# A hybrid encoder layer on one core: the forgetting-attention stage reordered, a fifth head's queries and keys computed in the first stage, and the small loads of that stage issued by GpSimd

## The chip, the cores and the metric

The kernel runs on one NeuronCore of a Trainium2 chip. The metric is the device time of one execution in microseconds (us); the time of a kernel is the median of its runs. The engines are named as the profile names them: PE is TensorE (PEld its weight loads), DVE VectorE, ACT ScalarE, POOL GpSimd, SP SyncE.

## The reference

One layer is computed for two groups of tokens together: 512 prompt tokens and 8 x 16 sample tokens, 640 columns in all, with a model width of 2048.

```
z = x @ w_in                       # queries, keys, values, gates, DeltaNet inputs, merge gates
branch A (FoX, 8 heads of 128):    s = q k^T * scale + (c_q - c_k), causal; softmax; p v
    sample tokens attend to a cache of 512 past rows per group and to themselves
branch B (gated DeltaNet, 8 heads): conv, normalise, chunked delta rule
y = sig(gA) * (A_out * silu(gate)) @ w_out_fox + sig(gB) * (B_out * silu(gate)) @ w_out_gdn
x1 = LayerNorm(alpha * x + y @ w_out)
out = x1 + sigmoid(x1 @ w_pl_gate) * RMSNorm(p @ w_pl_proj)
```

The keys, values, log forget values and DeltaNet states are outputs too. Everything is float32.

## The kernel before, in words

**Matrix products.** A float32 product is made of three products in the fast float32 format: weights and inputs are each split into a rounded part (`wh`, `xh`, cast by ACT) and a remainder (`wl`, `xl`, subtracted by DVE), and the sum wh·xh + wh·xl + wl·xh is accumulated. The 640 columns are two halves of 320. A block of 128 output rows is called a column of weights: 16 contraction steps x 2 halves x 3 products = 96 matmuls of 128x320, at lines L396 and L397 (`column`). Two columns can instead be made as a pair at L474 (`pair`), by a scheme with seven products in place of eight: 7 products x 8 steps x 3 = 168 matmuls of 128x320 in place of 192. A pair needs sums of weight tiles, made by DVE (L319). For some later pairs the sums are made ahead by POOL from tiles that SP loads and stores again (`weight_sums`, L291, L295, L301).

**Stages.** `front` computes the first columns, all gates and values, 22 merge gates, and queries and keys of four heads (`APART`), the last of these as pairs; queries and keys go to DRAM (`qkd`). `phase_fox` has the rest of the columns (`column`), among which the eight attention heads are spread, and the projection `proj` of the per-layer embedding. `phase_gdn` has the DeltaNet heads, spread among the columns that they need, and `tail` has the output projections.

**Order.** The program is written out by hand: the matmuls of the columns go on, and after every second step `tick` runs through the lanes, which are generators that emit a part of a head and say how long to wait. A model of the engines (`saw`) keeps `self.clock`, the time of PE by the model; a lane goes on when the clock has reached its time, when `self.now` (the count of ticks) allows, and when the PSUM banks of the stage's small products (`sps`, three of them) are modelled as read (`banks_free`). `self.every = 2` lets a lane step on every second tick. A step that yields a negative number waits until the model has its engines done less 1.5 us.

**A head.** `fox_all` takes a head when its queries and keys are ready and the head before the last is done. `fox_in` loads the gate (`sg`) and the values (`vn`), and has POOL copy the sample queries into `qpad`. For each of four blocks of 128 prompt queries, `scores` makes the scores (L754 for the first block, L388 to L390 for the others), DVE adds the bias `nb`, ACT takes exp; `fox_step` scales them (`softmax2`), transposes them (L726), copies them (L729), multiplies them with the values (L742). `fox_dec` does the sample tokens against the cache: scores with `kc` (L773) and with their own keys (L776), softmax, transposes (L793, L799), copies by ACT to `ppad` (L795) and `pn` (L801), products with `vc` (L813). `fox_out` transposes its result and stores the head.

**Loads.** All loads of this stage are issued by SP in one order with the weights (`wr`, L269): queries and keys (L1529), bias (L637, L639), gate (L665), values (L633), four tiles of 512 KB of the cache's keys and four of its values per head (L627). The tiles of `phase_fox` lie where those of `front` were, so its first memset and first loads wait until the last stores of `front` have landed.

Of the kernel before, what the change touches and what calls it, by code (L numbers as in the profile page):

```python
# [52 lines left out]
class Kernel:  # L53
# [9 lines left out]
    APART = 2, 3, 5, 6  # L63
    NG = 8
    PAIR0, PAIRS = 6, NG + 2 + FRONT // 2 + len(APART)
    BETWEEN = 3, 6
# [6 lines left out]
    def __init__(self, tc, ins, outs):  # L73
        self.clock, self.busy, self.wrote, self.paced = 0.0, [0.0, 0.0, 0.0], {}, False
        self.tc, self.nc, self.i, self.o = tc, tc.nc, ins, outs
        self.lanes, self.every = [], 2
        self.banks, self.read, self.nbanks = [], {}, 3
        self.now = 0


    def saw(self, ins):


        if ins.engine not in ENGINES or not ins.outs or not hasattr(ins.outs[0], "ap"):
            return
# [22 lines left out]
    def watch(self, gen):  # L108
# [7 lines left out]
        return abs(n), t + (0.25 if n > 0 else -1.5)  # L116
# [513 lines left out]
    def load_v(self, h):  # L630

        self.vn[h] = self.zt([P, 5, P], "vn", 2)
        self.nc.sync.dma_start(out=self.vn[h], in_=self.vd[:, :, h * P:(h + 1) * P].rearrange("t p d -> p t d"))  # L633

    def load_bias(self, h):
        nb = self.zt([P, T], "nb", 2)
        self.nc.sync.dma_start(out=nb, in_=bcast(self.rd[h], T, P))  # L637
        nbd = self.zt([P, NPT], "nbd", 2)
        self.nc.sync.dma_start(out=nbd, in_=bass.AP(self.sfd.tensor, self.sfd[h * 8].offset,  # L639
# [3 lines left out]
    def softmax1(self, xs, n):  # L643
# [3 lines left out]
        nm = self.zt([P, 1], "nm", 6)  # L647
        nc.vector.reduce_max(out=nm, in_=xs[:, 0:n], axis=AX.X, negate=True)
        sm = self.zt([P, 1], "sm", 6)
# [9 lines left out]
    def fox_in(self, h, q):  # L659

        nc = self.nc
        if h == 0:
            self.load_bias(0)
# [3 lines left out]
        if h == 0:  # L667
            for j in range(4):
                self.load_kv(0, "k", j)

# [12 lines left out]

    def fox_all(self):


        flow = [None] * 4
        for h in range(H):
            while h not in self.heads or self.heads[h][2] > self.now or min(self.outdone, self.decdone) < h - 2:
# [3 lines left out]
            q, k, _ = self.heads.pop(h)  # L693
            self.fox_in(h, q)
            if h == 0:
                yield 5
                for j in range(4):
                    self.load_kv(0, "v", j)
                yield 4
            parts = None  # L700
            for i in range(4):
                self.fox_step(flow)
                flow[0] = h, i, self.scores(h, i, q, k, parts)
# [14 lines left out]
    def fox_step(self, flow):  # L718

        nc = self.nc  # L720
        spread = weigh = None
        if flow[1]:
            h, i, (xs, _) = flow[1]
# [7 lines left out]
        if flow[0]:  # L731
            h, i, (xs, sm) = flow[0]
            self.softmax2(xs, P * (i + 1), sm)
            weigh = flow[0]
        if flow[2]:
            h, i, pT = flow[2]
            if i == 0:
                self.og = self.zt([P, T], "og", 2)
            vn, sl = self.vn[h], slice(i * P, (i + 1) * P)
            ops = self.sps()  # L740
            for kb in range(i + 1):
                nc.tensor.matmul(ops[:, 0:P], vn[:, kb, :], pT[:, kb * P:(kb + 1) * P], start=(kb == 0), stop=(kb == i))  # L742
            nc.vector.tensor_tensor(out=self.og[:, sl], in0=ops[:, 0:P], in1=self.sg[h][:, sl], op=ALU.mult)
            if i == 3:
                self.outs["gens"].append(self.fox_out(h, self.sg[h], self.og))
        flow[:] = None, weigh, spread, None

    def scores(self, h, i, q, k, parts):
# [9 lines left out]
        xs = self.zt([P, NPT], "xs", 3)  # L758
# [5 lines left out]
    def fox_dec(self, h, q, k):  # L764
# [12 lines left out]
        xd = self.zt([P, T], "xd")  # L777
# [12 lines left out]
        yield -2  # L790
        pt = self.dps()
# [6 lines left out]
        pt = self.sps()  # L798
        nc.tensor.transpose(pt[:, 0:P], xd[:, NPT:T], self.ident)  # L799
        pn = self.zt([P, P], "sq", 2, "pn")  # L800
        nc.scalar.copy(out=pn, in_=pt[:, 0:P])  # L801
        yield 4
# [418 lines left out]
    def run(self, ctx):  # L1221
# [18 lines left out]
        self.qkd = {(h, i): dr([P, T], F32, name=f"qkd{h}{i}") for h in (0, *self.APART) for i in range(2)}  # L1240
# [7 lines left out]
        self.outs, self.decs = self.lane(), self.lane()  # L1248
# [35 lines left out]
    def front(self, work):  # L1284
# [179 lines left out]
        def weights():  # L1464
# [3 lines left out]
            yield from self.weight_sums([t[:, x:x + 256] for t in ws for x in (0, 256)], slice(0, 12), (6, 4, 2))  # L1468
# [33 lines left out]
    def phase_fox(self, work):  # L1502
# [6 lines left out]
        self.heads, self.sg = {}, {}  # L1509
# [4 lines left out]
        ws = self.zt([P, 1024], "ws")  # L1514
        self.sums["gens"].append(self.weight_sums([ws[:, x:x + 256] for x in range(0, 1024, 256)], slice(12, 13),
                                                  (9, 7, 5, 20)))
        for h in range(H):
            qk = []
            if h in self.BETWEEN:
                self.mcol("eacc")  # L1520
            for c in range(2):
                stored = (h, c) in self.qkd
                if not stored:
                    acc = self.column()[0]
                self.until(lambda: min(self.qkdone) >= h - 2)
                x = self.zt([P, T], "qk"[c], 2)
                qk.append(x)
                if stored:
                    nc.sync.dma_start(out=x, in_=self.qkd[h, c])  # L1529
                    continue  # L1530
                for hf in range(2):
                    sl = slice(hf * HALF, (hf + 1) * HALF)
# [941 lines left out]
```

## Time and profile before

| | us |
|---|---|
| three runs | 2170.36, 2176.83, 2175.85 |
| median | 2175.85 |
| profiled execution | 2173.18 |
| its span, first to last instruction | 2171.3 |
| PE busy in the span | 2149.0 |

The profile's page has the busy time of each engine, the span in 40 slices, the DMA queues, the chain of work that ended last, the costliest groups of instructions and the DMA issues. A row of a window gives, after its limits and its length, the busy us and the number of instructions of PE, PEld, DVE, ACT and POOL, then the granted PE clock, the mean busy share of the 16 DMA engines and GB/s. A row of a timeline gives start, duration, engine, line, operation, tiles, and in brackets how long the engine had been idle and what ended it. `front` ends and `phase_fox` begins at 721.92 us of the span; `phase_fox` ends near 976 us.

### The profile page before, as it was taken

The page shows a single profiled execution, that of the slowest core. Times are in us where ns is not written, and L with a number is a line of the kernel's source. Part 1 is how long each engine was busy: PE and PEld are TensorE (multiplying, and loading weights), DVE is VectorE, ACT ScalarE, POOL GpSimd, SP SyncE. Part 2 cuts the span into 40 slices and gives each one's busy share as a digit, 9 for nine tenths or more (in the row PEclk, how much of TensorE's full clock was granted, in tenths as well). Part 3 has the DMA queues.
Part 4 walks back from the last instruction along what each step waited for, and adds up shares of the span by engine and source line. Part 5 has one row for each costly group of instructions (what it writes and reads, how often), then busy time and mean ns, then how long its engine had stood idle before and what let it go on. Part 6 is the DMA issues. An engine that isn't in the chain of part 4 may idle for free.

```text
span 2171.3 us, 41951 instructions
## 1 busy us (share of the span) xinstructions
PE 2149.0 (99%) x15438; PEld 2082.3 (96%) x15438; DVE 1566.0 (72%) x3207; ACT 1007.3 (46%) x2213; POOL 401.9 (19%) x596
## 2 busy tenths in 40 slices
PE   9999999999999999999999999999999999999998
PEld 7799999999999998899999999999999999999998
DVE  5877776767776565566478677766757787789987
ACT  4344443443444343353655566655443343354544
POOL 0022233323330101002334333332000000021100
PEclk9999999999999999999999999999999999999999
DMA  6356656666554899869978778878567656673465
GB/s 235 101 184 202 189 182 199 198 199 194 184 180 158 276 325 344 314 199 291 241 179 199 180 188 194 189 182 248 161 229 260 209 171 202 201 276 122 153 227 173
DMA packets 240670, 452.65 MB, mean 208 GB/s; under 512 B 38920, under 2 KB 122504, under 8 KB 240464
## 3 DMA queue, kind: packets, MB, share of 16 engines
q1 hardware_dynamic: 224912, 421.64, 59.5%
q0 software_dynamic: 15552, 28.32, 8.0%
q8 instruction: 122, 2.00, 0.4%
q14 instruction: 84, 0.69, 0.1%
HBM read 353.48 MB, written 96.38 MB: 207 GB/s over the span
## 4 chain that ended last, share of the span: by engine, by line
PE 91%; DVE 3%; DMA 3%; ACT 1%; SPq 0%; issue 0%; POOL 0%; ACTq 0%; DVEq 0%; POOLq 0%
PE g L474 44%; PE g L396 18%; PE g L397 18%; PE g L440 2%; PE s L974 1%; PE s L742 1%; PE s L813 1%; PE s L773 1%; DMA ws138b<-ws 0%; PE s L440 0%; PE s L1168 0%; DMA nb<-rd 0%; DVE sx L1006 0%; DVE sx L1004 0%; PE s L726 0%
## 5 line engine op out<-in xcount | busy, mean ns | idle before, releaser
L329 ACT CAST wh<-wr 128x512 fp32r<-128x512 f32 x624 | 381.2, 619 | 288.7 <-PE g L474 109.5
L335 DVE TENSOR_TENSOR wl<-wr,wh 128x512 fp32r<-128x512 f32 x516 | 358.3, 708 | 183.5 <-ACT wh L329 173.7
L474 PE MATMUL g<-xh,wh 128*128 128x320 f32 (+1 forms) x1296 | 402.9, 311 | 2.7 <-ACT m L1278 1.6
L474 PE MATMUL g<-xl,wh 128*128 128x320 f32 (+1 forms) x1296 | 401.2, 310 | 0.6 <-DVE xl L371 0.6
L474 PE MATMUL g<-xh,wl 128*128 128x320 f32 (+1 forms) x1296 | 401.4, 310 | 0.0
L396 PE MATMUL g<-xh,wh 128*128 128x320 f32 (+1 forms) x960 | 313.0, 326 | 0.7 <-ACT wh L329 0.7
L396 PE MATMUL g<-xh,wl 128*128 128x320 f32 (+1 forms) x960 | 297.1, 309 | 0.8 <-DMA wl<-in_w 0.7
L396 PE MATMUL g<-xl,wh 128*128 128x320 f32 (+1 forms) x960 | 297.2, 310 | 0.4 <-DVE xl L371 0.4
L397 PE MATMUL g<-xh,wh 128*128 128x320 f32 x960 | 297.3, 310 | 0.0
L397 PE MATMUL g<-xl,wh 128*128 128x320 f32 x960 | 297.0, 309 | 0.0
L397 PE MATMUL g<-xh,wl 128*128 128x320 f32 x960 | 296.7, 309 | 0.0
L474 PEld LDWEIGHTS g<-xh,wh 128*128 128x128 f32 x1296 | 243.9, 188 | 4.3 <-ACT m L1278 2.1
L474 PEld LDWEIGHTS g<-xl,wh 128*128 128x128 f32 x1296 | 243.7, 188 | 1.1 <-DVE xl L371 1.1
L474 PEld LDWEIGHTS g<-xh,wl 128*128 128x128 f32 x1296 | 244.1, 188 | 0.0
L474 PE MATMUL g<-t,wh 128*128 128x320 f32 (+1 forms) x1088 | 241.4, 310 | 0.0
L335 DVE TENSOR_TENSOR wl<-sr,wh 128x512 fp32r<-128x512 f32 x200 | 147.9, 759 | 98.6 <-ACT wh L329 97.6
L295 POOL TENSOR_TENSOR ws<-ws 128x171 f32<-128x171 f32 (+2 forms) x152 | 116.7, 768 | 541.5 <-DMA ws<-in_w 535.7
L396 PEld LDWEIGHTS g<-xh,wh 128*128 128x128 f32 x960 | 180.9, 188 | 11.9 <-issue 7.1
L474 PEld LDWEIGHTS g<-t,wh 128*128 128x128 f32 x1088 | 181.9, 188 | 0.6 <-issue 0.3
L396 PEld LDWEIGHTS g<-xh,wl 128*128 128x128 f32 x960 | 180.6, 188 | 1.4 <-DMA wl<-in_w 1.0
L397 PEld LDWEIGHTS g<-xh,wh 128*128 128x128 f32 x960 | 181.0, 189 | 0.9
L396 PEld LDWEIGHTS g<-xl,wh 128*128 128x128 f32 x960 | 180.9, 188 | 1.0 <-DVE xl L371 1.0
(440 smaller groups left out, 4148.8 us busy)
## 6 DMA issues: line engine op xcount, KB each, us to landing
wr<-in_w SPq DMA_DIRECT2D x252, 512.0 KB
wl<-in_w POOLq DMA_DIRECT2D x108, 256.0 KB, 5.8
kc<-in_kc SPq DMA_DIRECT2D x32, 512.0 KB
vc<-in_vc SPq DMA_DIRECT2D x32, 512.0 KB
sr<-in_w SPq DMA_DIRECT2D x25, 512.0 KB
ws<-in_w SPq DMA_DIRECT2D x96, 128.0 KB
sb<-in_w SPq DMA_DIRECT2D x80, 128.0 KB
md<-m SPq DMA_DIRECT2D x32, 320.0 KB
```

What stands on the lines that cost most here:

```text
L295: nc.gpsimd.tensor_tensor(out=o, in0=x, in1=y, op=op)
L329: nc.scalar.copy(out=hi, in_=src)
L335: nc.vector.tensor_tensor(out=lo, in0=src, in1=hi.bitcast(F32), op=ALU.subtract)
L396: nc.tensor.matmul(ps[0], whl[w], xhl[o][:, a], start=(first and x == 0), stop=(last and x == 2))
L397: nc.tensor.matmul(ps[1], whl[w], xhl[o][:, b], start=(first and x == 0), stop=(last and x == 2))
L440: nc.tensor.matmul(ps, x[:, sl], w, start=(s == 0 and n == 0), stop=(s == 15 and n == 2))
L474: nc.tensor.matmul(ps, a[:, w], b, start=(k == 0 and n == 0 and not more), stop=(k == last and n == 2), skip_group_check=True)
L742: nc.tensor.matmul(ops[:, 0:P], vn[:, kb, :], pT[:, kb * P:(kb + 1) * P], start=(kb == 0), stop=(kb == i))
L773: nc.tensor.matmul(s1[32 * j:32 * j + 32, :], self.qpad[:, 2 * j + par, :], kc[:, (j % 2) * NPT:(j % 2 + 1) * NPT], start=(par == 0), stop ...
L813: nc.tensor.matmul(od[32 * j:32 * j + 32, 0:P], self.ppad[:, c, 2 * j + par, :], vc[:, o:o + P], start=False, stop=(par == 1 and c == 3), ...
L974: nc.tensor.matmul(pp[:, o:o + 256].rearrange("p (a b) -> p a b", a=2), kq[:, 0, x], kq[:, :, x], start=True, stop=True)
```

## The change

- `APART` has five heads (1, 2, 3, 6, 7) in place of four; `front` has one pair more, `phase_fox` two columns fewer. Queries and keys of heads 4 and 5 are computed in `phase_fox` (`JOBS`) and go to DRAM as well. Head 0's were stored at the start, as before.
- The loads of `q`, `k`, `nb`, `nbd`, `sg` and `vn` are issued by POOL. The cache tiles, weights and stores stay with SP.
- At the start of `phase_fox`, head 0's queries, keys, bias and its eight cache tiles, and head 1's queries and keys, are all asked for at once. Head 0 may begin 5 us of the model's clock after that, a later head 7 us after its load, and at least 21.5 us (`PACE`) after the head before.
- In this stage a lane may step on every tick (`every = 1`) and a negative yield waits until the engines are done by the model (`lead = 0`).
- The step of a head is cut differently: transposes, then the product with the values, then the new scores, then the scaling of the scores before. The end of the sample tokens is a lane of its own (`fox_dec2`), with the small transpose and its copy `pn` ahead of the large ones.
- The 13th of the sums of weights made by POOL is made in `front` in place of `phase_fox`. `proj` starts with three tiles for its results and gets four more when head 7 is done.
- The model no longer counts DMA issues as work (`saw`).

The diff, cut to its core:

```diff
-    APART = 2, 3, 5, 6
     NG = 8
+    APART = 1, 2, 3, 6, 7
-    BETWEEN = 3, 6
+    PACE = 21.5
+    JOBS = 4, 5, None, None
...
-        return abs(n), t + (0.25 if n > 0 else -1.5)
+        return abs(n), t + (0.25 if n > 0 else -self.lead)
...
-        self.nc.sync.dma_start(out=self.vn[h], in_=self.vd[:, :, h * P:(h + 1) * P].rearrange("t p d -> p t d"))
+        self.nc.gpsimd.dma_start(out=self.vn[h], in_=self.vd[:, :, h * P:(h + 1) * P].rearrange("t p d -> p t d"))
...
-        nc.sync.dma_start(out=self.sg[h], in_=self.sgf[h])
+        nc.gpsimd.dma_start(out=self.sg[h], in_=self.sgf[h])
...
+    def load_qk(self, h):
+        qk = []
+        for c in range(2):
+            qk.append(self.zt([P, T], "qk"[c], 2))
+            self.nc.gpsimd.dma_start(out=qk[c], in_=self.qkd[h, c])
+        self.heads[h] = *qk, self.clock + (7 if h else 5)
+
     def fox_all(self):
-        flow = [None] * 4
+        flow, begun = [None] * 5, 0.0
+        self.load_qk(0)
+        self.load_bias(0)
+        for j in range(4):
+            self.load_kv(0, "k", j)
+        self.load_qk(1)
+        for j in range(4):
+            self.load_kv(0, "v", j)
         for h in range(H):
-            while h not in self.heads or self.heads[h][2] > self.now or min(self.outdone, self.decdone) < h - 2:
+            while h not in self.heads or max(self.heads[h][2], begun + self.PACE) > self.clock or min(self.outdone, self.decdone) < h - 2:
...
-                    while self.qkdone[1] < h - 1:
+                    while self.qkdone[1] < h - 1 or h + 1 not in self.kept:
                         yield 1
                     self.load_bias(h + 1)
+                    if h:
+                        self.load_qk(h + 1)
...
+        self.decs2["gens"].append(self.fox_dec2(h, xd))
+
+    def fox_dec2(self, h, xd):
+        nc = self.nc
+        pt = self.sps()
+        nc.tensor.transpose(pt[:, 0:P], xd[:, NPT:T], self.ident)
+        pn = self.zt([P, P], "sq", 2, "pn")
+        nc.scalar.copy(out=pn, in_=pt[:, 0:P])
         pt = self.dps()
...
+        self.every, self.lead = 1, 0.0
         work["gens"].append(self.fox_all())
```

**How the order moves.** First SP, where `front` ends and `phase_fox` begins (`qkd` and `out_fk` are the last stores of `front`). Before:

```order
L1457 DMA qkd_194<-m_1170 128x640
L1459 DMA out_fk<-m_1170 128x640
L1457 DMA qkd_193<-m_1169 128x640
L1529 DMA q<-qkd_185 128x640
L1529 DMA k<-qkd_186 128x640
L269 DMA wr<-in_w 128x1024 x2
L637 DMA nb<-rd 128x640
L639 DMA nbd<-sfd 128x1x512
L665 DMA sg<-sgf_169 128x640
L633 DMA vn<-vd 128x5x128
L627 DMA kc<-in_kc 128x1024 x4
```

Now:

```order
L1468 DMA qkd_200<-m_1176 128x640
L1470 DMA out_fk<-m_1176 128x640
L1468 DMA qkd_199<-m_1175 128x640
L628 DMA kc<-in_kc 128x1024 x4
L628 DMA vc<-in_vc 128x1024 x4
L270 DMA wr<-in_w 128x1024 x3
```

The small loads have left SP's order, and eight cache loads stand ahead of three weight loads. They stand on POOL now, at the same place:

```order
L1517 MEMSET qpad 128x256
L1518 MEMSET ppad 128x1024
L683 DMA q<-qkd_185 128x640
L683 DMA k<-qkd_186 128x640
L638 DMA nb<-rd 128x640
L640 DMA nbd<-sfd 128x1x512
L683 DMA q<-qkd_187 128x640
L683 DMA k<-qkd_188 128x640
L664 DMA sg<-sgf_169 128x640
L634 DMA vn<-vd 128x5x128
L667 COPY qpad<-q 128x4x16 x2
```

Head 0's queries and keys stand behind both memsets of POOL; before, SP issued these loads, and the memsets stood on another engine. On PE the first scores of head 0 (`s<-k,q`) stood behind 120 matmuls of columns from the start of `phase_fox`. Now, with the first row the last matmul of `front`, and 42 matmuls of columns from the second row to the row ahead of the scores:

```order
L475 MATMUL g<-xh,wl 128x320
L397 MATMUL g<-xh,wh 128x320
L398 MATMUL g<-xh,wh 128x320
...
L397 MATMUL g<-xh,wl 128x320
L398 MATMUL g<-xh,wl 128x320
L761 MATMUL s<-k,q 128x128
L397 MATMUL g<-xh,wh 128x320
L398 MATMUL g<-xh,wh 128x320
```

So the first head stands 78 matmuls earlier. Between the first scores of one head and those of the next there were 84, 84, 84, 120, 84, 84 and 120 matmuls of columns; there are now 108, 66, 84, 78, 84, 78 and 78.

On ACT, within a head, before (`pn` behind the two copies to `ppad`):

```order
L795 COPY ppad<-s 128x16x16 x2
L801 COPY pn<-s 128x128
L729 COPY pT<-s 128x128
L650 ACTIVATE xs,sm<-xs,nm 128x384
L329 CAST wh<-wr 128x512
```

Now:

```order
L805 COPY pn<-s 128x128
L810 COPY ppad<-s 128x16x16 x2
L735 COPY pT<-s 128x256
L651 ACTIVATE xs_9381,sm<-xs_9381,nm 128x512
L827 COPY on<-s 128x128
```

The copy that empties the PSUM bank `s` now goes ahead of the two that empty another bank.

More of the change, by code (lines that the diff above doesn't have):

```diff
@@ L81, in saw @@
     def saw(self, ins):
-        if ins.engine not in ENGINES or not ins.outs or not hasattr(ins.outs[0], "ap"):
+        if ins.engine not in ENGINES or "DMA" in type(ins).__name__ or not ins.outs or not hasattr(ins.outs[0], "ap"):
             return
@@ L693, in fox_all @@
             q, k, _ = self.heads.pop(h)
+            begun = self.clock
             self.fox_in(h, q)
[L695 to L699, printed above, removed]
             parts = None
             for i in range(4):
-                self.fox_step(flow)
-                flow[0] = h, i, self.scores(h, i, q, k, parts)
+                self.fox_step(flow, (h, i, q, k, parts))
                 if i == 0:
@@ L1239, in run @@
         self.sgd = self.sgf[H:]
-        self.qkd = {(h, i): dr([P, T], F32, name=f"qkd{h}{i}") for h in (0, *self.APART) for i in range(2)}
+        self.qkd = {(h, i): dr([P, T], F32, name=f"qkd{h}{i}") for h in range(H) for i in range(2)}
         self.vd = dr([5, P, 1024], F32, name="vd")
@@ L1513, in phase_fox @@
         self.vn = {}
[L1514 to L1519, printed above, removed]
-                self.mcol("eacc")
[L1521 to L1532, printed above, removed]
-                    if c == 0:
-                        nc.scalar.mul(x[:, sl], acc[hf], FOX_SCALE)
-                    else:
-                        nc.scalar.copy(out=x[:, sl], in_=acc[hf])
-                if c:
-                    nc.sync.dma_start(out=self.o["fk"][h], in_=x)
-            self.heads[h] = *qk, self.now + (9 if stored else 1)
@@ L1563, in phase_fox @@
         nc.sync.dma_start(out=self.sqd, in_=self.eacc)
+        self.every, self.lead = 2, 1.5
     def mcol(self, tag, **kw):
@@ L1779, in e_evac @@
         if n == 0:
[L1781 removed]
+            self.until(lambda: self.qkdone[1] == 7 and not self.sums["gens"])
             self.eacc = self.zt([P, T], "eacc")
[L1783 to L1784 removed]
+            tiles = [self.zt([P, 1024], "kc", 4, "e")[:, 0:T] for _ in range(4)]
+            self.e_tiles, self.q_tiles = tiles[0:3], [tiles[3]] * 2
             self.esq = None
+        if n == 3:
+            self.until(lambda: self.decdone == 7)
+            tiles = [self.zt([P, 1024], "vc", 4, "e")[:, 0:T] for _ in range(4)]
+            self.e_tiles, self.q_tiles[1] = [*self.e_tiles, *tiles[0:3]], tiles[3]
         e = self.e_tiles[n % len(self.e_tiles)]
@@ L2383, in _layout @@
     rest = iter(m[nf:nf + 3])
-    for h in range(1, H):
-        bl += [next(rest) for _ in range(h in Kernel.BETWEEN)]
-        if h not in Kernel.APART:
-            bl += [bq[h], bk[h]]
+    for h in Kernel.JOBS:
+        bl += [next(rest)] if h is None else [bq[h], bk[h]]
     bl += rest
```

93 lines of the change are left out of this document (49 added, 44 removed).

## The prediction

> **What bounds the kernel now.** I read the busy times first, then the chain that ended last, then the windows stage by stage.
>
> ```profile
> PE 2149.0 (99%) x15438; PEld 2082.3 (96%) x15438; DVE 1566.0 (72%) x3207; ACT 1007.3 (46%) x2213; POOL 401.9 (19%) x596
> PE 91%; DVE 3%; DMA 3%; ACT 1%; SPq 0%; issue 0%; POOL 0%; ACTq 0%; DVEq 0%; POOLq 0%
> 400.00:450.00 50.00, 50.00 (x343) 50.00 (x342) 35.34 (x48) 20.25 (x38) 15.43 (x15) 1.00 0.61 195
> 736.00:950.00 214.00, 211.01 (x1913) 192.76 (x1912) 131.50 (x313) 87.65 (x229) 16.28 (x30) 1.00 0.87 311
> 850.00:900.00 50.00, 48.42 (x446) 43.40 (x444) 32.92 (x82) 18.74 (x52) 4.57 (x8) 1.00 1.01 360
> ```
>
> PE is busy 99% of the span and holds 91% of the chain. So the time is PE's work plus PE's waits, and every other engine counts only where PE waits for it. The third row (a stretch of `front`) gives the price of a matmul of 128x320: 50 us / 343 = 0.146 us. The fourth and fifth rows are the attention stage: PE idles 3.0 us of 214 by this count, and the DMA engines are nearly full (share 0.87, in one stretch 1.01, at 360 GB/s). The waits of PE in this stage, and the one late load that the chain runs through there:
>
> ```profile
> PE s L754 <- ACT pn L801: 0.8, 1, 0.8
> PE s L388 <- ACT pn L801: 0.8, 1, 0.8
> PE s L388 <- DVE xd L780: 0.7, 2, 0.5
> PE s L754 <- ACT k L1536: 0.3, 1, 0.3
> PE s L388 <- ACT pT L729: 0.3, 1, 0.3
> 850.12 9.15 DMA nb<-rd
> ```
>
> They come to 2.9 us. The reader should see that this is nearly all that a better order of the heads can win: the heads already hide behind the columns.
>
> **The change part by part.** *Matmuls removed.* Queries and keys of one more head are made as a pair: 168 matmuls in place of 192. 24 x 0.146 = **-3.5 us**. The number and shapes of all other matmuls stay as they were, so this is all of PE's work that goes. The pair's extra sums and casts are DVE and ACT work in `front`, where DVE is busy 35.34 of 50 us and ACT 20.25: covered, and if they were not, the loss would show as PE waits, of which 400 to 450 has none.
>
> *Waits in the heads.* `pn` now goes ahead of the two `ppad` copies, which is what the two rows of 0.8 us wait for; fewer columns of queries and keys are left to empty (0.3); with `lead = 0` a step stands where the model has the engines done. The 0.7 us on `xd` stay likely, since the first head still has its cache scores and the next large scores without columns between. I take away 2.9 - 0.7 = 2.2 and add about 1.0 for what the view doesn't count: it shows a matmul as 0.31 us long though the next starts after 0.146, so each of six waits is some 0.16 longer than shown. **-3.2 us**, bounds 0 (new waits as large as the old ones, since 66 to 84 matmuls now lie between most heads) and -4.
>
> *Head 0 moved forward.* This is the large term on the other side. Here are the end of `front` on PE, SP's last store, POOL's memsets and the first scores before:
>
> ```profile
> 721.92 0.31 PE L396 MATMUL g<-xh,wh 128*128 128x320 f32 x1
> 724.43 0.32 SPq L1457 DMA_DIRECT2D qkd<-m  x1
> 726.66 0.32 SPq L1529 DMA_DIRECT2D q<-qkd  x1
> 726.71 0.31 POOL L1506 MEMSET qpad<- 128x256 f32 x1 [77.27 <-DMA qkd<-m]
> 726.96 0.95 POOL L1507 MEMSET ppad<- 128x1024 f32 x1
> 729.65 0.89 POOL L672 COPY qpad<-q 128x64 f32<-128x64 f32 x2 [1.73 <-DMA q<-qkd]
> 739.53 0.38 PE L754 MATMUL s<-k,q 128*128 128x128 f32 x2
> ```
>
> Call 721.92 zero. The memory of `phase_fox` is free when the last store of `front` has landed: 726.71 - 721.92 = 4.8. Before, the first scores stood at 17.6 (120 matmuls x 0.146) and found their loads long landed. Now they stand behind 42 matmuls: 42 x 0.146 = 6.1. And the loads that they need are issued by POOL behind its two memsets, which end at 726.96 + 0.95 - 721.92 = 6.0. What an issue by POOL costs is shown by the only DMAs that POOL issues in this kernel, the weight remainders of the DeltaNet stage (first row: the issue, least, median and most in ns; second: from issue to landing in us):
>
> ```profile
> L342 POOL DMA_DIRECT2D wl<-in_w x108: 847/865/1194, 1012.6 to 1493.2; - x108
> DMA to landing us min/median/max: 3.6/5.8/9.2
> ```
>
> The queries are issued at 6.0, the keys at 6.0 + 0.87 = 6.9, and the keys land at 6.9 + 5.8 = 12.7. PE reaches them at 6.1: **+6.5 us** of waiting. The bounds: as quick as SP's load of the same tile, 729.65 - 726.66 = 3.0, gives 9.9, a wait of 3.7; the slowest landing, 9.2 (the bias load in the chain took 9.15 too), gives 16.1, a wait of 9.9. I take the median, because eight cache loads of 512 KB are asked for from 4.8 on and fill the DMA engines as they are filled where those 108 ran. Nothing can run ahead of it: PE goes in order, the columns stand behind the scores, and DVE and ACT wait for the columns' banks. Head 0's bias, third on POOL, lands some 0.9 us after the keys and delays DVE, not PE: the next scores are 24 matmuls (3.5 us) on. `qpad` follows eight issues (6.0 + 8 x 0.87 = 13.0), and its reader, PE's cache scores, stands after the wait too.
>
> The Trainium skill, "DMA: Bandwidth & Descriptors", in the section on the anatomy of a DMA issued by GpSimd, gives 2.0 us plus the bytes at 436 GB/s; for 320 KB that is an estimate of 2.75 us, with which the wait would be 3.5 and the sum 3.0 us lower. The 108 rows above, of 256 KB, disagree with it in a filled stage, and the measured ones decide.
>
> *The clock behind the wait.* One wait of PE in the trace was followed by a slower granted clock, another wasn't:
>
> ```profile
> 1447.48 0.38 PE L1196 MATMUL s<-vr,uu 128*128 128x128 f32 x1 [1.92 <-DVE uu L1074]
> 1448.00:1451.00 3.00, 3.00 (x13) 3.00 (x13) 2.90 (x8) 2.16 (x4) 0.17 (x1) 0.50 1.08 275
> 1451.00:1455.00 4.00, 4.00 (x31) 3.99 (x30) 3.65 (x15) 0.41 (x2) 0.69 (x1) 0.94 0.91 206
> 99.77 0.42 PE L474 MATMUL g<-xh,wh 128*128 128x320 f32 x1 [1.65 <-ACT m L1278]
> 99.00:102.40 3.40, 2.63 (x18) 2.63 (x19) 2.79 (x5) 0.65 (x2) 0.00 (x0) 1.00 0.41 154
> ```
>
> After 1.92 us idle the clock was 0.50 for 3 us and 0.94 over the next 4: 3 x 0.50 + 4 x 0.06 = 1.7 us lost. After 1.65 us it stayed at 1.00. A wait of 6.5 us is longer than both: **+1.7 us**, bounds 0 (as behind the 1.65) and twice that (it is three times the 1.92). The Trainium skill, "TensorE: Matmul & The Clock Gate", in its part on the clock gate, says that the clock is halved after an idle window of about 3.4 us and comes back after as long a busy one; the rows agree with the half clock, and by that rule the price lies between the one I take and its double.
>
> *At nothing.* The 48 DMAs that POOL now issues are 48 x 0.87 = 42 us of an engine that is busy 16.28 us of 214; uncovered, they would delay `qpad`. The 13th sum of weights falls into the end of `front`, where POOL is idle:
>
> ```profile
> 650.00:700.00 50.00, 50.00 (x342) 50.00 (x342) 34.30 (x50) 20.22 (x37) 0.00 (x0) 1.00 0.40 135
> 731.44 4.67 SPq L627 DMA_DIRECT2D kc<-in_kc  x4
> 737.62 3.33 SPq L627 DMA_DIRECT2D vc<-in_vc  x4
> ```
>
> The three weight loads that now stand behind eight cache loads wait 4.67 + 3.33 = 8.0 us longer for their issue; by the order of SP four halves of columns (4 x 48 matmuls = 28 us) are issued ahead of them, which covers that and 4.2 MB in front (12 us at 360 GB/s). Without this cover it would be PE that waits for `wh`. The end of the stage is covered too: behind the last product of head 7 there are 25 us of columns ahead of the next stage's first small product, where there were 35. Fewer result tiles in `proj` and shared buffers hang on stores that have several columns' time. The DeltaNet stage keeps its work, but its order shifts a little where it follows the sums; its waits may fall better or worse, by about the 1.92 + 1.7 of the event above either way. I take 0.
>
> *The sum*: -3.5 - 3.2 + 6.5 + 1.7 = **+1.5 us**. On the profiled execution, 2173.2 (span 2171.3 and 1.9 around it), that is 2174.7; this execution lies 2.7 under the median of the runs, on which it would be 2177.4. I give the middle, **2176**.
>
> **The rivals.** *Faster: the loads come early.* For: SP's load of the same tile took 3.0 us, and POOL's queue is empty before. Against: the engines fill up just then. The wait is 3.7, short of a drop in the clock, the waits in the heads go by the full 4, and the DeltaNet event (3.6) isn't there again: -3.5 - 4 + 3.7 - 3.6 = -7.4, or 2166 on the profiled execution. Without the wait for head 0 at all it would be 2162, but the landing at 4.8 and any load after it leave no room for that.
>
> *Slower: the DMA engines set the pace of the heads.* The tiles that it counts:
>
> ```profile
> kc<-in_kc SPq DMA_DIRECT2D x32, 512.0 KB
> vc<-in_vc SPq DMA_DIRECT2D x32, 512.0 KB
> nb<-rd SPq DMA_DIRECT2D x8, 320.0 KB
> L754 PE MATMUL s<-k,q x16: 272/275/377, 739.5 to 912.4; 128*128 128x128 f32 x16
> ```
>
> Per head 8 x 0.524 + 6 x 0.328 (`q`, `k`, `sg`, `vn`, `nb`, the result) + 0.26 (`nbd`) + about 0.9 of weights and 0.25 of stored queries and keys = 7.6 MB. Heads came every (912.4 - 739.5) / 7 = 24.7 us; with 12 matmuls fewer between them (94 to 82) that is 24.7 - 1.8 = 22.9 us, or 332 GB/s. The stretch 850 to 900 carried 360, the whole stage only 311. From 332 GB/s downwards the cache tiles come late: at 311 a head needs 24.4 us, 1.5 late, x 7 = 10.5 us, on top of the sum: 2185. Against it: no row of before has PE waiting for a cache tile, though the share was 1.01.
>
> *The heads are denser on paper only.* Waits as large as the old ones come back (-3.2 becomes 0), and head 0 waits 9.9 with the double price of the clock: -3.5 + 9.9 + 3.4 = +9.8, or 2183.
>
> **How the numbers follow.** What a measurement of this kernel can tell from no change is about 0.3%, 6.5 us. The forecast, head 0's wait against the saved matmuls and waits, has 0.50; it lies within 6.5 us on both sides, and its own range is 2169 to 2181. Early loads have 0.25 (faster), the DMA engines 0.16 and the denser heads 0.09 (both slower). So faster 0.25, same 0.50, slower 0.25. The range that holds it 8 times in 10 reaches into both: 2166 to 2185.
>
> **What would show it.** Right: PE's longest wait of the stage stands at the first scores of head 0 (`s<-k,q`), 3.7 to 9.9 us, ended by a DMA of `k` or `q`, with a granted clock under 1.00 in the next 3 us; 24 matmuls fewer; the rows on `pn` gone; `phase_fox` shorter by two columns. Wrong: the first scores start without a wait, or the landing from POOL takes under 3 us; PE waits on `kc` or `vc` (the DMA rival); the rows of POOL's issues are much longer than 0.9 us; or the waits of the later stages change by more than 4 us.

## The result, and the profile after

The changed kernel takes **2197.0 us** (2194.8 to 2198.5), the kernel before beside it 2174.6: a ratio of 1.0108, with a 95% interval of 1.0093 to 1.0124. It is 22.4 us slower, and the range of 2166 to 2185 did not hold it. The profiled execution took 2198.52 us, its span is 2196.7, that is 25.4 more than the span before. Three executions of the kernels below, of 2305 to 3485 us at a granted clock of 0.56 to 0.85, are left out of the medians.

I cut the span at five places: the first pair of `front`, the first column of `phase_fox`, the first small product of the DeltaNet stage (`s<-rt,cb`), the half pairs behind that stage, and the columns behind those. Here are three of these windows before (start and end; length; busy us and number of PE, PEld, DVE, ACT, POOL; granted clock, DMA share, GB/s):

```profile
721.92:986.50 264.58, 261.59 (x2259) 242.51 (x2258) 161.29 (x369) 108.08 (x268) 23.11 (x45) 1.00 0.85 297
986.50:1578.05 591.55, 587.12 (x4464) 564.30 (x4464) 413.24 (x1274) 335.21 (x911) 185.87 (x317) 1.00 0.81 203
1578.05:1636.53 58.48, 57.84 (x423) 55.84 (x422) 37.19 (x83) 29.43 (x69) 0.61 (x1) 1.00 0.72 241
```

And all five of after:

```profile
99.98:746.52 646.54, 645.25 (x4392) 644.20 (x4393) 464.14 (x621) 270.67 (x506) 178.84 (x176) 1.00 0.61 193
746.52:994.70 248.18, 235.86 (x2061) 216.10 (x2060) 153.15 (x360) 104.03 (x256) 39.30 (x77) 0.98 0.86 303
994.70:1596.89 602.19, 591.59 (x4427) 566.45 (x4425) 413.19 (x1269) 337.38 (x910) 184.15 (x317) 0.99 0.79 199
1596.89:1662.61 65.72, 62.19 (x469) 58.05 (x468) 38.81 (x89) 30.66 (x72) 0.61 (x1) 1.00 0.64 219
1662.61:2196.70 534.09, 526.09 (x3558) 523.69 (x3556) 435.06 (x754) 230.73 (x401) 29.06 (x64) 1.00 0.59 200
```

- `front` (99.77 to 721.92 before, 622.15 us): +24.4, the 168 matmuls of the new pair at 0.146 us. As forecast.
- The attention stage: -16.4. Two columns fewer are 192 x 0.146 = 28.0, so 11.6 us were lost here.
- The DeltaNet stage and the half pairs: 650.0 became 667.9, **+17.9**, with the same work in it but for the place of the cut: the stage's first small product stands 6 matmuls (0.9 us) earlier in the changed kernel, so 0.9 of the 17.9 belong to the attention stage. PE's idle time in the two rose from 5.1 to 14.1 us. The other 8.8 count as busy: the clock fell to 0.99, and small gaps hide in the 0.31 us that the view gives a matmul.
- Everything behind: the same.

So most of the loss stands in a stage that the change does not touch. Now the attention stage of after, PE's rows of the view of waits (who waited, for whom: us in total, times, longest):

```profile
PE s L761 <- issue: 8.5, 1, 8.5
PE g L397 <- ACT m L1575: 1.7, 1, 1.7
PE g L397 <- DVE e L1796: 1.0, 1, 1.0
PE s L780 <- issue: 0.5, 1, 0.5
PE s L389 <- DVE og L746: 0.4, 1, 0.4
PE s L389 <- DVE xd L787: 0.3, 1, 0.3
```

Both rows on `pn` are gone. One wait of 8.5 us stands at head 0's first scores, and two new ones of 1.7 and 1.0 us in `proj`. Around the long one: POOL's issues and PE's first scores from the timeline, the landing of `k` in this stretch (least, median, most of two loads; the least is head 0's), and four windows from PE's last column to past its end:

```profile
752.55 0.81 POOL L683 DMA_DIRECT2D q<-qkd  x1
753.34 0.59 POOL L683 DMA_DIRECT2D k<-qkd  x1
761.34 0.77 PE L761 MATMUL s<-k,q 128*128 128x128 f32 x2 [8.47 <-issue]
...
DMA to landing us min/median/max: 7.7/11.2/14.7
...
752.60:757.10 4.50, 0.26 (x2) 0.00 (x0) 0.00 (x0) 0.00 (x0) 4.50 (x9) 1.00 0.95 350
757.10:761.30 4.20, 0.00 (x0) 0.00 (x0) 0.00 (x0) 0.00 (x0) 1.48 (x4) 0.50 1.05 379
761.30:767.30 6.00, 5.96 (x23) 6.00 (x24) 2.31 (x6) 1.94 (x5) 1.19 (x2) 0.50 1.00 276
767.30:771.00 3.70, 3.70 (x28) 3.69 (x27) 2.10 (x7) 1.11 (x3) 0.35 (x1) 0.99 1.02 394
```

The keys are issued 6.8 us into the stage and land 7.7 later, while the DMA engines have a share of 0.95 to 1.05. PE, there after 6.1, waits 8.5. The view names nothing that ended this wait ("issue"), but the keys land at 753.34 + 7.7 = 761.0, 0.3 us ahead of the scores. The clock is halved 4.5 us into the wait and stays so for 6.0 us of work: 3.0 us lost.

In the DeltaNet stage and the half pairs, PE's longest wait was 1.9 us before (on `uu`, shown in the prediction). The longest after are

```profile
PE s L1207 <- DVE rp L1203: 2.6, 2, 2.2
PE g L397 <- DMA wl<-in_w: 2.6, 1, 2.6
PE g L475 <- ACT wh L330: 1.9, 1, 1.9
```

and the clock fell to half for 3.4 us behind three of the waits there (windows of 10 us, from 1050, 1285 and 1430 us, have 0.83); before, behind one.

### The profile page after: what moved, and what is told of

The parts are those of the page before. It is cut to its first block, busy times and chain, and to the rows that moved or that the text cites. A ratio compares the mean times of both kernels' runs of the same rounds, so it can differ in the third digit from the quotient of the medians.

```text
span 2196.7 us, 42035 instructions
## 1 busy us (share of the span) xinstructions
PE 2157.4 (98%) x15414; PEld 2085.4 (95%) x15414; DVE 1577.2 (72%) x3222; ACT 1016.2 (46%) x2219; POOL 434.2 (20%) x644
## 4 chain that ended last, share of the span: by engine, by line
PE 85%; DVE 6%; DMA 5%; ACT 2%; issue 1%; SPq 1%; POOL 0%; ACTq 0%; POOLq 0%; DVEq 0%
PE g L475 44%; PE g L397 16%; PE g L398 15%; PE g L441 2%; DVE sx L1017 1%; DVE sx L1015 1%; PE s L742 1%; DMA lanes<-ld 1%; PE s L824 1%; PE s L780 1%; PE s L985 1%; DMA ws138b<-ws 0%; DMA wr<-in_w 0%; PE s L441 0%; PE s L1179 0%
## 5 line engine op out<-in xcount | busy, mean ns | idle before, releaser
L398 PE MATMUL g<-xh,wh 128*128 128x320 f32 x928 | 289.1, 312 | 0.0
L398 PE MATMUL g<-xh,wl 128*128 128x320 f32 x928 | 288.1, 310 | 0.0
L398 PE MATMUL g<-xl,wh 128*128 128x320 f32 x928 | 288.0, 310 | 0.0
L475 PEld LDWEIGHTS g<-xh,wh 128*128 128x128 f32 x1328 | 250.0, 188 | 7.5 <-ACT wh L330 2.1
L336 DVE TENSOR_TENSOR wl<-sr,wh 128x512 fp32r<-128x512 f32 x208 | 155.4, 765 | 103.7 <-ACT wh L330 102.4
L296 POOL TENSOR_TENSOR ws<-ws 128x171 f32<-128x171 f32 (+2 forms) x140 | 110.0, 786 | 525.3 <-DMA ws<-in_w 520.6
L330 ACT CAST wh<-sr 128x512 fp32r<-128x512 f32 x208 | 125.0, 618 | 136.9 <-PE g L475 104.7
L397 PEld LDWEIGHTS g<-xh,wh 128*128 128x128 f32 x928 | 176.3, 190 | 11.6 <-issue 7.3
## 6 DMA issues: line engine op xcount, KB each, us to landing
kc<-in_kc SPq DMA_DIRECT2D x32, 512.0 KB, 10.5
```

What stands on the lines that cost most here:

```text
L296: nc.gpsimd.tensor_tensor(out=o, in0=x, in1=y, op=op)
L330: nc.scalar.copy(out=hi, in_=src)
L336: nc.vector.tensor_tensor(out=lo, in0=src, in1=hi.bitcast(F32), op=ALU.subtract)
L397: nc.tensor.matmul(ps[0], whl[w], xhl[o][:, a], start=(first and x == 0), stop=(last and x == 2))
L398: nc.tensor.matmul(ps[1], whl[w], xhl[o][:, b], start=(first and x == 0), stop=(last and x == 2))
L475: nc.tensor.matmul(ps, a[:, w], b, start=(k == 0 and n == 0 and not more), stop=(k == last and n == 2), skip_group_check=True)
```

## The experiments

Each kernel was timed against the kernel before on the same chip, whose median lay between 2172.2 and 2173.7 us.

**The DeltaNet stage: one tick.** The stage's lanes step only where the count of ticks is even (`self.every = 2`). Ordered by instruction, its first difference is at head 1's scores: 696 column matmuls of the stage stand ahead of them before, 720 after; over the stage its small products stand some 20 matmuls (about 3 us) later on average. One tick more at its start gives the changed kernel the order of the kernel before there, instruction for instruction, and gives the kernel before that of the changed one. So I ran both:

```diff
     def phase_gdn(self, conv, work):
+        self.now += 1
```

> The changed kernel with one edit: the count of ticks gets one more at the start of phase_gdn. Nothing before that stage moves, and from there the order of PE is word for word that of the kernel before. Theory (the DeltaNet stage lost 17.8 us, 10.6 in the stage and 7.2 in the half pairs behind it, because its lanes step on every second tick and now start on the other one): those 17.8 us come back, 2197.0 - 17.8 = 2179 us, and the waits at 1051.5, 1285.9, 1433.7 and 1642.5 us are gone. Rival (the loss is of data or of loads: buffers, stores and weights reach the stage in another state than before): the order alone brings less than 5 us back, 2192 us or more.

> The kernel before with the same single edit, so that its DeltaNet stage has the order of the changed kernel, with all of the attention stage as it was. Theory (the tick's parity alone makes the loss): 17.8 us slower than before, 2192 us. Rival (the loss comes from what the changed attention stage leaves behind): within 5 us of before, 2175 to 2180 us.

Measured: the changed kernel with the tick **2184.4 us** (ratio 1.0054, 1.0039 to 1.0069), 12.6 less; the kernel before with it **2182.5** (1.0047, 1.0030 to 1.0064), 9.6 more. The windows of the DeltaNet stage and the half pairs, of the changed kernel with the tick:

```profile
997.47:1589.51 592.04, 587.21 (x4466) 564.25 (x4464) 413.19 (x1274) 334.98 (x911) 184.34 (x317) 1.00 0.81 202
1589.51:1648.00 58.49, 57.84 (x424) 55.84 (x423) 37.41 (x84) 29.63 (x70) 0.61 (x1) 1.00 0.73 242
```

and of the kernel before with it:

```profile
985.81:1579.67 593.86, 587.84 (x4426) 563.36 (x4425) 412.96 (x1268) 336.76 (x910) 184.45 (x317) 1.00 0.80 201
1579.67:1645.40 65.73, 62.20 (x468) 58.06 (x467) 38.84 (x89) 30.68 (x72) 0.61 (x1) 1.00 0.63 218
```

650.5 us and 659.6, against 650.0 and 667.9. So the order makes the loss of this stage in the changed kernel; in the kernel before it costs 9.6, which is neither what the theory gave (17.8) nor the rival (under 5). Laid side by side, matmul by matmul, the two executions with this same order part at three places: at 1054 us of the changed kernel (PE waits 2.6 us for `wl`, in the other 1.1, and the clock halves), at 1156 (1.2 us more) and at 1288 (1.9 us more, for `rp`, and the clock halves). These make up the 8 us. Why `wl` and `rp` come later there stays open. With the tick, 11.5 us stay lost. The attention stage took 251.1 us in that execution and 248.2 without the tick; 0.9 of this is the place of the cut, and 1.7 another half clock, 3.4 us long, behind the first wait in `proj` (its windows of 5 us from 935 and 940 have a clock of 0.89 and 0.77).

**Head 0's place.** If the 8.5 us and the half clock are the price of an early start, a later one saves them:

```diff
-        self.heads[h] = *qk, self.clock + (7 if h else 5)
+        self.heads[h] = *qk, self.clock + (7 if h else 20)      # 14 in the second kernel
```

> The changed kernel with head 0 held back: it may begin 20 us of the model's clock after its loads are asked for in place of 5, so 150 matmuls (21.9 us) stand ahead of its first scores in place of 42. The DeltaNet stage keeps the changed kernel's order. Theory (the 8.6 us of waiting at head 0's first scores and the half clock behind it, 6.3 us of work at half speed = some 3.1 us, are the price of the early place): both go, 2197.0 - 11.7 = 2185 us, less what the last heads lose, which stand 42 and 30 matmuls apart. Rival (the loads by GpSimd or the full DMA engines delay the stage as a whole, and the wait only moves to a later head): 2194 us or more, with new waits on k, q, kc or nb.

> The changed kernel with 14 in place of 5: 102 matmuls (14.9 us) stand ahead of head 0's first scores; the keys landed about 14.7 us after the stage's start in the changed kernel. By this shift the stage ends on the other tick, so the DeltaNet stage gets the order of the kernel before with no other edit. Theory (wait and clock of head 0 11.7 us, parity 17.8 us, and the two add): 2197.0 - 11.7 - 17.8 = 2167.5 us, faster than the kernel before by 7. Rival (head 0's place is not free: the heads are squeezed at the end and lose it again; or the parity is not the cause): 2175 us or more.

Measured: **2212.9** (1.0184, 1.0169 to 1.0200) and **2197.5** (1.0113, 1.0098 to 1.0128). The theory fell: they are 28 and 30 us above what it gave. ACT's timeline with 14:

```profile
759.80 0.77 ACT L1538 ACTIVATE qk<-g 128x320 f32<-128x320 f32 x2 [3.11 <-PE g L398]
777.36 0.62 ACT L330 CAST wh<-wr 128x512 fp32r<-128x512 f32 x1 [16.79 <-DMA wr<-in_w]
...
780.44 0.61 ACT L675 CAST kh<-k 128x512 fp32r<-128x512 f32 x1
```

Head 0's keys landed at 760.0, but ACT stands 16.8 us at a weight that SP asked for behind eight cache tiles, and the cast of the keys stands behind that weight's cast. PE waits 14.9 us for it (12.0 with 20), and the clock is at half for 17.1 us. In the changed kernel the cast stood ahead of the late weight, and the wait for the keys hid it. The squeezed heads at the end cost about 6 us more: going by the starts of the matmuls, waits of 2.8, 2.3, 1.6, 1.2 and 1.1 us from 912 to 957 with 14, where the changed kernel has its 2.7 in `proj`. The clock is at half there for another 6.8 us, which costs 3.4.

**Who asks, and for how much.** Three kernels with the tick: head 0's value tiles and head 1's queries and keys asked for later in the program; head 0's queries, keys and bias by SP ahead of the caches; both. A fourth has all small loads by SP.

```diff
-        self.load_qk(1)                                          # late: behind head 0's second scores
-        for j in range(4):                                       # late: behind head 0's first scores
-            self.load_kv(0, "v", j)
```

```diff
-            self.nc.gpsimd.dma_start(out=qk[c], in_=self.qkd[h, c])
+            (self.nc.gpsimd if h else self.nc.sync).dma_start(out=qk[c], in_=self.qkd[h, c])
-        self.nc.gpsimd.dma_start(out=nb, in_=bcast(self.rd[h], T, P))
+        (self.nc.gpsimd if h else self.nc.sync).dma_start(out=nb, in_=bcast(self.rd[h], T, P))
```

> The changed kernel with the tick edit (2184.4 us; wait at head 0's first scores 8.7 us, phase_fox 251.1 us), and of the early loads only the keys' cache left early: head 0's four value tiles are asked for behind its first scores, head 1's queries and keys behind its second. Theory A (the wait is for bytes: 4.2 MB of caches fill the DMA engines beside the small loads): 2.7 MB less ahead, the wait falls to 3 to 6 us, phase_fox to 244 to 247, 2177 to 2181 us. Theory B (the wait is the place of the issue: GpSimd behind two memsets and its own queue): the wait stays at 8 to 9 us, 2184 us.

> The changed kernel with the tick edit, and head 0's queries, keys and bias alone issued by SP, ahead of the eight cache tiles; all other small loads stay with GpSimd and all bytes are the same. Theory B (place of the issue): the keys land as fast as SP's did in the kernel before (3.0 us behind the issue), the wait falls from 8.7 to about 3 us, no half clock, phase_fox 242, 2175 us. Theory A (the engines are full, whoever issues): the weights that stand behind the caches land near 30 us after the stage's start in any case (the kernels with head 0 held back waited for them until then), so PE waits for those in place of the keys: the first wait falls, a new one of 3 to 6 us on wh or kh comes, 2180 us or more.

> Both edits: head 0's queries, keys and bias by SP ahead, value tiles and head 1's loads late. If A and B each hold a part, the gains add: wait at the first scores at most 3 us, no wait on weights, phase_fox 240 to 242 us, 2173 to 2175 us. If A alone holds, as with late caches alone; if B alone, as with SP first alone.

> The changed kernel with the tick edit (2184.4 us, phase_fox 251.1 us), and every small load of the attention stage issued by SP at the same point of the program; all other orders are the same. Theory (who issues decides only who is late first): the 8.7 us at head 0's first scores falls to under 3.5 us, but waits of the same sum come on caches and weights behind, phase_fox 249 to 253 us, 2182 to 2187 us. Rival (issuing by GpSimd costs in itself, in every head): phase_fox under 245 us, 2179 us or less.

Measured: **2184.6**, **2185.6**, **2183.3** and **2185.0 us** (ratios 1.0059, 1.0059, 1.0049, 1.0059, each ±0.0017 or less), all like the 2184.4 without these edits. The waits tell more than the times. With the caches late:

```profile
PE s L760 <- issue: 8.6, 1, 8.6
```

With SP first (ACT's row on a weight, and PE's over 1 us):

```profile
ACT wh L330 <- DMA wr<-in_w: 6.2, 1, 6.2
...
PE s L803 <- DVE xd L657: 4.0, 1, 4.0
PE s L761 <- DMA q<-qkd: 2.4, 1, 2.4
PE g L397 <- ACT m L1575: 1.6, 1, 1.6
PE s L780 <- DMA kc<-in_kc: 1.4, 1, 1.4
PE g L397 <- DVE e L1797: 1.1, 1, 1.1
```

So the wait at the first scores depends on who asks and where: it falls from 8.6 to 2.4 with SP ahead. The first kernel does not decide between the theories, because its edit hardly moved the bytes. SP's value tiles in the changed kernel, and with the caches "late":

```profile
753.13 2.26 SPq L628 DMA_DIRECT2D vc<-in_vc  x4
754.80 3.24 SPq L628 DMA_DIRECT2D vc<-in_vc  x4
```

They stand behind head 0's first scores in the program, but SP asked for them 4 to 7 us before PE ran those scores (761.9), with two weight loads ahead of them; only head 1's 0.66 MB of queries and keys really came behind the landing of head 0's keys. And with SP first two things changed at once: the engine that asks, and the 2.1 MB of key tiles that no longer stand ahead of the keys. No run separates them, so theory A (bytes) is not excluded for this wait. What is won there is paid again: ACT waits for a weight, DVE's `xd` comes late, PE waits 4.0 and 1.4 us. With both edits it is `kc` (3.7 us), with all by SP `vn` (5.8). That is what theory A said for the second kernel, on other tiles.

**The bytes themselves.** To the kernel with both edits:

```diff
+        if h == 0 and j:
+            store[h, j] = store[h, 0]
+            return
```

> The kernel with both edits (SP first, caches late; 2183.3 us, phase_fox 249.1 us), but head 0 loads one of its four key tiles and one of its four value tiles, and all four products of each read that one: 3.1 MB fewer at the stage's start, so the sample tokens of head 0 get a wrong cache and everything else is kept. Theory (what is left of the loss is a debt of the DMA engines: they are full from 5 us on, whatever the order, and PE pays at whichever tile comes late): 3.1 MB at 360 GB/s = 8.7 us of transfers less, the waits for kc at head 0 and head 1 (1.9, 1.9 and five of 0.5 to 0.8 us) and the half clock behind them go, phase_fox 240 to 242 us, 2174 to 2176 us. Rival (the engines are not it: the place of head 0 and the order of DVE and ACT are): phase_fox stays over 246 us, 2180 us or more.

Measured: **2177.0 us** (1.0021, 1.0012 to 1.0031), 6.3 less than with all tiles, where 7 to 9 were expected; the attention stage took 243.0 in place of 249.1. No row of PE on `kc` is left. So more than half of the 11.1 us by which the kernel with both edits is over the kernel before goes with those six loads: a debt of the DMA engines at the stage's start. Whether it is their bytes or their number was not separated, and 4.4 us stay.

**Is there an order that pays the debt?** First, to both edits, one weight load ahead of the key tiles as well (`yield 2` before they are asked for), and head 0 at 8 in place of 5. In the other three the heads also stand at a distance of 20.5, so that none is squeezed, with head 0 at 8, at 14, and at 14 with the changed kernel's own loads:

```diff
-    PACE = 21.5
+    PACE = 20.5
```

> As the kernel with both edits, and in addition one weight load ahead of the keys' cache, and head 0 beginning 8 us of the model's clock after its loads (66 matmuls, 9.6 us, ahead of its first scores); the DeltaNet stage gets the order of the kernel before by this shift, without the tick edit. Theory (the price of head 0 is the order of the loads at the stage's start, and the pair and the better heads are worth what was worked out, 3.5 + 2.6): no wait over 1 us at head 0, phase_fox 237 to 239 us, 2167 to 2170 us, faster than the kernel before by 3 to 6. Rival (a start that lacks 8 us of DMA time can't be mended by order, a wait on kc, wh or vn comes in its place): 2175 us or more.

> The same with 8 in place of 14: head 0 starts 66 matmuls into the stage and the last heads stand 60 and 66 apart. Theory as before, with waits of 2 to 4 us for head 0's key tiles left: phase_fox 243 to 246 us, 2176 to 2180 us. Rival: as in the kernel with 8 and a distance of 21.5 (248.6 us), 2183 us or more.

> The kernel with both edits and one weight load ahead of the key tiles, head 0 beginning 14 us of the model's clock after its loads, and a least distance of 20.5 in place of 21.5, so that the heads stand 48 to 66 matmuls apart and none is squeezed to 30. DeltaNet order as in the kernel before. Theory (the late start lets the engines catch up, and the closer heads cost nothing): no wait over 1 us at head 0, phase_fox 240 to 243 us, 2172 to 2176 us. Rival (a head needs 7.6 MB, and 60 matmuls apart that is 21 us of PE time, 357 GB/s: the engines have no slack to pay back the debt, and kc or vc come late in the later heads): phase_fox 246 us or more, 2180 us or more.

> The changed kernel's own loads (GpSimd for all small loads, eight cache tiles ahead of the weights), with the tick edit, 14 in place of 5 and 20.5 in place of 21.5. Theory (the order of the loads decides): ACT waits for the weights behind the caches and holds the cast of head 0's keys, as with 14 alone (15 us, half clock behind it): phase_fox 252 to 258 us, 2186 to 2192 us. Rival (the squeezed heads at the end made that kernel slow, not the loads): phase_fox under 245 us, 2179 us or less.

Measured: **2184.5** (1.0051, 1.0035 to 1.0066), **2179.7** (1.0035, 1.0021 to 1.0048), **2173.0** (1.0000, 0.9991 to 1.0009) and **2185.1** (1.0059, 1.0044 to 1.0074). The first missed its theory by 14 us, with waits on head 0's key tiles and the squeezed end; the second is at the upper end of its own; the third came out at the time that its theory gave, with an attention stage of 239.0 us, though a wait of 2.0 us was left in head 0 (behind a weight for which ACT waited 6.6), where it had none over 1. The fourth has the third's place and distance with the changed kernel's own loads, and PE's long wait is there again:

```profile
ACT wh L330 <- DMA wr<-in_w: 16.3, 1, 16.3
...
PE s L389 <- ACT kh L675: 14.4, 1, 14.4
```

So the order of the loads makes 12.1 us of difference at this place. The distance matters as much: with 21.5 the same place and loads took 2197.5, 12.4 more. The squeezed end is where they stand: from 900 to 960 us PE's busy time is 51.2 us with 21.5, with 6.8 us at half clock, and 59.6 with 20.5, without a half clock.

Could it beat the kernel before? Five more tries, written as head 0's place and the distance: all small loads by SP, 14/20.5; GpSimd as in the third kernel, 16/20; all by SP, 16/20; then 14/20.5 by SP with the queries and keys of heads 1 to 7 by GpSimd, or of heads 2 to 7 (head 1's by SP, ahead of `vc`):

> The kernel of 14 and 20.5 (2173.0 us, phase_fox 239.0 us), with all small loads issued by SP at the same points of the program. SP waits there for free weight buffers, so head 1's loads can't run ahead as they do on GpSimd. Theory (head 1's early loads, 2.2 MB = 6 us at 360 GB/s, are what makes the weights late, for which ACT waits 6.6 us and PE then 2.1): the waits of 1.6, 2.1 and 0.7 us go, phase_fox 235 to 237 us, 2169 to 2171 us. Rival (the bytes are needed anyway, and SP's queue makes something else late, as vn was with all loads by SP): phase_fox 239 us or more, 2173 us or more.

> The kernel of 14 and 20.5 with 16 and 20: 126 matmuls ahead of head 0's first scores, heads 54 to 66 apart, GpSimd's loads as there. Theory (debt at the start): another 3.5 us for the engines to catch up, the waits for kc and behind the late weight shrink from 4.4 us to under 2, phase_fox 236 to 238 us, 2170 to 2172 us. Rival (density): the heads are as near as a head's bytes allow, new waits on kc or vc in heads 2 to 6, phase_fox 240 us or more, 2174 us or more.

> All small loads by SP, 16 and 20. Theory (both the debt and head 1's early loads count): phase_fox 233 to 236 us, 2167 to 2170 us, faster than the kernel before by 3 to 6 us, which is the pair's 3.5 us and the saved waits. Rival: as h1_sp14 or slower, 2173 us or more.

> All small loads by SP, 14 and 20.5 (2178.3 us, phase_fox 243.4 us), but queries and keys of heads 1 to 7 by GpSimd. Theory (the gain was there, and late keys hid it): the waits of 5.3, 0.9 and 1.4 us for k go and the half clock behind them, phase_fox 235 to 237 us, 2169 to 2172 us, 2 to 5 us faster than the kernel before. Rival (the engines are full, and taking the keys earlier makes weights or vc late): phase_fox 239 us or more, 2173 us or more.

> The same, but head 1's queries and keys by SP, asked for behind head 0's first scores and ahead of its value tiles, so that they don't compete with head 0's key tiles and the first weights. Theory: as the kernel with GpSimd for head 1 or up to 2 us less, 2168 to 2171 us. Rival: a new wait in head 1, 2173 us or more.

Measured: **2178.3** (1.0027, 1.0016 to 1.0038), **2185.6** (1.0056, 1.0040 to 1.0072), **2179.8** (1.0032, 1.0017 to 1.0047), **2172.0** (0.9999, 0.9991 to 1.0008) and **2174.5** (1.0004, 0.9995 to 1.0013). The first three went as their rivals had it or worse: PE waited 5.2 us for head 1's keys; 7.5 us behind a weight for which ACT had waited 8.6 (not for `kc` or `vc`, as that rival had it); 2.9 us for keys. In the last two the waits for keys went, as the theory said, and one of 4.0 and 3.7 us on head 1's key tiles came, where the first rival had named weights or `vc`; the time of the first is at the upper end of its theory's range, that of the second above it. In time they can't be told from the kernel before. No version is faster than it beyond its interval. What is left in the best of them (14/20.5, queries and keys by GpSimd), PE's rows over 0.3 us, and its attention stage:

```profile
PE s L780 <- issue: 4.0, 1, 4.0
PE g L398 <- DVE e L1797: 0.4, 1, 0.4
...
100.13:747.16 647.03, 645.35 (x4392) 644.14 (x4393) 465.90 (x621) 271.22 (x506) 178.80 (x176) 1.00 0.61 193
747.16:987.13 239.97, 235.00 (x2066) 214.96 (x2065) 152.28 (x361) 103.69 (x256) 20.32 (x43) 0.99 0.87 313
```

One wait of 4.0 us is left, at head 1's key tiles, with 6.8 us of half clock behind it (3.4 lost). `front` and attention together take 887.0 us, before 886.7. That wait and its clock, 7.4 us together, are more than the pair saves (3.5); a kernel without them, in which the gain would show, was not reached.

## Why the prediction was wrong, step by step

- *Matmuls removed, -3.5*: right. `front` grew by 24.4, as 168 x 0.146 = 24.5 says.
- *Head 0, +6.5 (3.7 to 9.9)*: the mechanism was right, with PE there after 6.1 us and the keys issued at 6.8 (6.9 forecast). The mis-sized term is the landing: 7.7 us, where the median of 108 loads, 5.8, stood in the sum. Measured 8.5, inside the bounds. The estimate of 2.75 us worked out from the Trainium skill, "DMA: Bandwidth & Descriptors", in the section on the anatomy of a DMA issued by GpSimd, is far from the 7.7 in this filled stretch.
- *The clock behind it, +1.7 (0 to 3.4)*: 3.0 us. The half clock lasted 6.0 us of work, not 3. The Trainium skill, "TensorE: Matmul & The Clock Gate", Part 1, has free-running windows of 3.4 us, of which one must be busy before the clock returns, so that between one and two pass; the 6.0 us agree with that. Its condition for the drop, an idle window of about 3.4 us, does not agree: the clock halved behind a wait of 1.92 us before, and behind waits of 2.6, 2.2 and 1.1 us in the DeltaNet stage of the changed kernel, and the measurement decides.
- *Waits in the heads, -3.2 (0 to -4)*: the rows on `pn` went, as said, but `proj` got two new ones of 1.7 and 1.0 us, where ACT and DVE empty a column's banks behind head 7's softmax. By the view the waits beside head 0's went from 2.9 to 3.9 us: +1.0, outside the bounds. "The end of the stage is covered too" is the step that failed here: it looked at the next stage's first product and not at `proj`.
- *Weight loads behind eight caches, covered by 28 us of columns*: this was not what made the changed kernel slow, but it was wrong. The prediction looked at PE's need for the weight, and not at ACT's, which comes earlier: ACT's instructions run in order, and whatever stands behind the cast waits with it, as the keys' cast did behind ACT's 16.8 us in the kernel with 14. The kernels with head 0 held back, the one with SP first, and two of the later ones with GpSimd (14/20.5 and 16/20) have this wait, 6.2 to 16.8 us on ACT; the one with both edits, where two weights are asked for ahead of the value tiles, and those with all loads by SP do not.
- *"The DeltaNet stage keeps its work ... I take 0"*, with 3.6 either way: **the step that failed**. The stage took 17.9 us more in the profiled execution, and its start on the other tick made 12.6 of the median, as the first experiment shows. With that mended the kernel took 2184.4, inside the range, but 11.5 over the kernel before beside it, where the sum said 1.5. With the measured sizes the sum is -3.5 + 1.0 + 8.5 + 3.0 = 9.0, and that execution has the further half clock (1.7): within the edited stage the waits in the heads are the term that is furthest off, by 4.2. That waits of later stages change by more than 4 us was named as what would make the prediction wrong; nothing in the trace of before could size it, but the order of the unedited stage could have been compared, and 3.6 either way was too narrow for an order that differs in every head.
- *The rivals*: "the loads come early" fell, with a landing of 7.7 and not 3.0. "The DMA engines set the pace of the heads" gave 2185 and is near to what is left without the tick, but by luck, not as it was told: the heads were not 1.5 us late each; the engines were in debt at the start. "Denser on paper" (2183) is the one whose mechanism is nearest to what is left: its wait of 9.9 and 3.4 for the clock were 8.5 and 3.0, and the waits in the heads did come back.

## What to carry to other kernels

Where an order is made by a counter or a planner, compare the order of the stages that are not edited too: here one tick of parity cost 12.6 us in a stage that nobody had edited, about as much as all the rest (11.5). Here the wait at the start of a stage with full DMA engines was a debt that showed: asking in another order moved it from keys to weights to caches, and only fewer loads, or more time ahead of the first use together with weights asked for early, took most of it away. Before calling a late load covered, look at each engine that touches it, not only at the one that needs the result. And an edit that places a load later in the program is not yet a load that is asked for later: read its issue in the trace.

## What was not expected of the hardware

The granted clock was halved while PE still waited, 4.5 us into the wait of 8.5, and stayed halved for 10.2 us in all; behind 14.9 us of waiting it stayed halved for 17.1. And 512 KB of the key cache took 10.5 us (median) from issue to landing in the changed kernel, and at the stage's start, with the engines' share near 1.00, the queries and keys by GpSimd 7.0 to 14.7 us. The issues of after (KB each, median us to landing):

```profile
wr<-in_w SPq DMA_DIRECT2D x251, 512.0 KB, 4.4
wl<-in_w POOLq DMA_DIRECT2D x108, 256.0 KB, 5.5
kc<-in_kc SPq DMA_DIRECT2D x32, 512.0 KB, 10.5
vc<-in_vc SPq DMA_DIRECT2D x32, 512.0 KB, 11.0
```

The same 512 KB took 4.4 us as weights, over the whole kernel, and 10.5 as cache tiles, which come four at a time. The trace holds the landing of only some of SP's loads, four of the 32 of each cache (9.2 to 17.3 us for the keys), so these two medians are rough; the GpSimd loads have all of theirs.
